# First modulation weights by column halves, sample rows as passes of their own on split weights, smaller transfers at the stage ends, and no table of delays, in a one-core decoder step

## The chip, the cores and the metric

The kernel runs on one core of a Trainium2 chip. The metric is the time of one execution in device microseconds (us). The core has TensorE (PE, with its weight loads shown apart as PEld), VectorE (DVE), ScalarE (ACT), GpSimd (POOL) and SyncE (SP); almost all transfers between DRAM and SBUF are issued on SP's queue.

## The reference, cut to what matters

One layer of a decoder is computed for a prompt of 2,048 tokens and for 8 decode samples of one token each, in float32. D is 1,024 and the FFN is 2,816 wide.

```python
mod = silu(c) @ w_ada + b_ada                 # c: 1 prompt row and 8 sample rows; w_ada is 1024 x 6144
sh1, sc1, ga1, sh2, sc2, ga2 = split(mod, 6)  # parts 0 to 5
h = rmsnorm(x, g_norm1) * (1 + sc1) + sh1
qkv, z, beta, a, aq, ak, av, iq, ik, iw = split(h @ w_in)     # w_in is 1024 x 3664
o_gdn = gated_delta_rule(silu(conv4(qkv)), a, beta)           # chunks of 64 tokens, 4 heads
o_att = attend(aq, ak, av, topk=256 of relu(iq . ik) * iw)    # 4 heads, 2 kv heads
x = x + ga1 * (concat(rmsnorm(o_gdn) * silu(z), o_att) @ w_out)
h2 = rmsnorm(x, g_norm2) * (1 + sc2) + sh2
gate, up = split(h2 @ w_ffn_in)
x = x + ga2 * ((silu(gate) * up) @ w_ffn_out)
y = rmsnorm(x, g_final)
```

The outputs are y for the prompt and for the samples, the new keys, values and index keys, and the new states of the convolution and of the delta rule.

## The kernel before, in words

**Products.** Every float32 product is made of three matmuls on operands that are split into a high and a low part: `mm3` (L206 to L208) issues high by high, high by low and low by high into one bank of PSUM. A weight tile of 128 x 512 is loaded raw into `wr` by `weights` (L175 to L199; the DMA is L188), copied to its high part on ACT (L189) and subtracted to its low part on DVE (L190); both parts lie in `wi`. The split tiles of w_in are written to DRAM (`kept`) in the first group and read from there in the three later ones. The banks of PSUM have names: `d` (four, the large products), `s` and `g` (two each).

**Tokens and groups.** The prompt is worked on in four groups of 512 tokens (`GT`), its 1,024 channels in eight blocks of 128 (`KB`, the index k). The samples ride along: in the projection of group 0, and in the FFN of the last group.

**Two phases.** Phase 1 goes through the groups: `project` (L676 to L768) makes the projection, `narrow` (L771) the per-head decay and index keys from a narrow product `smT`, and the chunks of the delta rule follow. Phase 2 (`phase2`, L1563) does the sparse attention (`indices` L1611, the searches for the top keys, `attends`), the samples' attention and `ffn` (L1784 to L2074). The FFN of a group is w_out, the norm, w_ffn_in by eleven pairs of 256 columns and w_ffn_out; the last group's stands alone at the end.

**Who sets the order.** PE takes the matmuls in the order in which they are written: `o` ties each matmul to the one before. That order comes from `weave` (L518), which runs several generators side by side: in phase 1 the delta rule (`chain`), the per-token work (`toks`) and the large products (`feeds`); in phase 2 `samples`, `indices`, `attends` and `feeds`. Each step of a generator yields its cost on PE, a time to wait before its next step, and the banks it uses. A planner's clock chooses the next step by those numbers. The table `DELAY` adds to that clock: for each generator it holds step numbers with a delay in us, 246 entries, 399 us in total (`feeds` 179, `chain` 69, `attends` 60, `samples` 41, `toks` 36, `indices` 14). It puts no wait into the program; it moves a step back in the order.

**The start.** `modulation` (L322) and `modulate` (L362) load the rows of w_ada for the shift and the scale (parts 0 and 1): eight DMAs of 128 x 1,024 for each (L347), with x of group 0 (L664) between them. The constants, the gate weights and the narrow weights follow on SP's queue (L360, L471 to L489), then the first w_in tiles. Each half of a part takes eight matmuls of 9 columns into two tiles of PSUM, which are copied to SBUF and turned by four times two matmuls (L388) that add the two tiles up; DVE adds the bias (L390). `hidden_T` (L436 to L445) turns x and applies scale and shift, k by k.

**The samples.** In the first three column blocks of group 0's projection the samples are the moving operand: two matmuls of 40 columns for each m and k (L714). In the other four blocks they are the stationary operand and the weight tile moves: two matmuls of 512 columns for each k (`mm_s`, L222 and L223). In the last group's FFN the raw weight tile is used, not the split one: `beside` (L1845) issues four matmuls, each with 32 columns of samples as stationary operand and 128 columns of the weight tile moving, into four strips of one bank. `tick` places them after a k-step. A ring of eight raw tiles (`wr`, `kT`, `V`) carries the weights there. `rows_s` (L1774) lays the samples' gates out to match.

**The stage ends.** The index keys are loaded by eight DMAs of 128 x 512 at the head of phase 2 (L1571). In a group's FFN x after w_out is stored to `x2_d` in one DMA of 2 MB (L1928), when w_out is done, and read again after the first columns of w_ffn_in (L2004). At the end `close` (L1969) scales the four token blocks by the last norm, 1,024 columns at a time on DVE, and stores each; then the samples are scaled and stored by four DMAs (L2073, L2074).

Of the kernel before, what the change touches and what calls it, by code (L numbers as in the profile page):

```python
# [20 lines left out]
try:  # L21
# [9 lines left out]
OP = mybir.AluOpType  # L31
# [32 lines left out]
DELAY = {  # L64
    "attends": {7: 1.43, 11: 5.06, 17: 0.31, 18: 6.69, 19: 0.55, 27: 0.49, 42: 13.11, 51: 1.2, 77: 3.19, 80: 2.39, 103: 0.94, 104: 0.27,
        105: 1.67, 124: 2.19, 125: 0.42, 126: 2.25, 135: 2.33, 137: 2.82, 138: 0.62, 144: 0.42, 149: 0.9, 150: 1.26, 151: 0.57, 152: 0.99,
        252: 0.46, 265: 1.77, 267: 1.16, 275: 0.26, 294: 1.69, 296: 0.59, 301: 1.84},
    "chain": {5: 0.24, 7: 1.06, 16: 2.03, 17: 0.26, 18: 1.33, 19: 0.98, 42: 0.55, 43: 1.2, 44: 0.61, 45: 0.44, 46: 1.05, 48: 0.61, 54: 0.55,
# [6 lines left out]
    "feeds": {1: 3.32, 161: 0.9, 166: 0.74, 242: 0.32, 281: 0.59, 362: 1.55, 363: 0.44, 365: 0.32, 425: 1.19, 431: 4.52, 503: 0.89, 538:  # L75
# [63 lines left out]
class K:  # L139
# [35 lines left out]
    def weights(self, src, key=None, raw=False):  # L175
# [6 lines left out]
        if raw:  # L182
            wr = raw()
        else:
            wr = self.wp.tile([128, 512], F32, name="wr", tag="wr", bufs=WR)
# [136 lines left out]
    def modulation(self):  # L322
# [20 lines left out]
        for part in range(2):  # L343
            if part:
                self.x0 = self.load_x(0)
# [1752 lines left out]
```

## Time and profile before

| | before |
|---|---|
| median of 3 runs | 3591.85 us (3581.23 to 3595.12) |
| the profiled execution, its own time | 3578.49 us |
| its span in the profile | 3576.7 us |
| mean granted clock of TensorE | 0.972 |
| busy share of PE, DVE, ACT, POOL | 94%, 58%, 41%, 16% |
| moved by DMA | 549.74 MB, 154 GB/s on average |

The profile is one execution, recorded by the hardware. A row of the timeline has the start, the duration, the engine, the line of the kernel, the operation, the output and the inputs with their shapes, and how often it stood there; in brackets is the idle time before it and what ended it. "x8" on a row means eight such instructions back to back under one stamp. "SPq" is the issue of a DMA on SP, "DMA" a transfer. A row of the waits has the waiting group, what it waited for, the us lost, how often, and the longest. Matmul ends are modelled, so the distance between two starts says more than a duration.

### The profile page before, as it was taken

Reading aid. Unit: us, or ns where it says so; the run is one execution under the profiler, and the core shown is the slowest. Engines: PE = TensorE matmul, PEld = TensorE weight load, DVE = VectorE, ACT = ScalarE, POOL = GpSimd, SP = SyncE. Lnnn points to the kernel's source line nnn. Section 1 sums busy time; section 2 is a strip of 40 time slices with the busy share of each in tenths; the row PEclk is TensorE's granted clock in tenths of the full one; section 3 lists DMA queues with packets and bytes.
Section 4 is the critical chain, followed back from the end, with each engine's and each line's share of the span. In section 5 each row is a group of like instructions: output and inputs, shape, how many; then the busy total and the mean of one; then the engine's idle time right before and its main releaser. Section 6 shows DMA issues by size and latency. Waiting matters only on the chain.

```text
span 3576.7 us, 62419 instructions
## 1 busy us (share of the span) xinstructions
PE 3367.3 (94%) x23125; PEld 2600.4 (73%) x23125; DVE 2065.2 (58%) x4465; ACT 1462.6 (41%) x2836; POOL 582.6 (16%) x550
## 2 busy tenths in 40 slices
PE   8999999999987889999999999999899999999997
PEld 5877777767765667777776777777677777677775
DVE  3656645636733657666678556667775744444434
ACT  3434323423432333454566545446564533322222
POOL 1001000101000113212220122222021122222223
PEclk8999999999998989999999999999999999999999
DMA  7765754765776344555464454235333333422222
GB/s 264 248 225 170 264 182 152 229 230 165 232 254 207 96 129 134 150 166 165 123 204 146 145 149 139 86 113 202 126 95 93 96 110 106 155 89 80 79 84 67
DMA packets 416877, 549.74 MB, mean 154 GB/s; under 512 B 49860, under 2 KB 287785, under 8 KB 416554
## 3 DMA queue, kind: packets, MB, share of 16 engines
q1 hardware_dynamic: 416562, 545.65, 48.0%
q8 instruction: 184, 3.01, 0.4%
q14 instruction: 131, 1.07, 0.1%
HBM read 441.78 MB, written 122.70 MB: 158 GB/s over the span
## 4 chain that ended last, share of the span: by engine, by line
PE 55%; DVE 5%; issue 3%; DMA 3%; ACT 2%; SPq 1%; POOL 1%; another core or an unknown queue 0%; DVEq 0%; ACTq 0%; POOLq 0%
PE d L206 14%; PE d L208 13%; PE d L207 13%; PE s L1665 3%; PE g L1727 3%; PE s L1710 2%; PE g L1845 1%; PE g L1739 1%; DVE wi L190 1%; ACT bias L1539 1%; DMA wr<-in_w_ffn_in_dram 1%; DMA wr<-in_w_ffn_out_dram 1%; ACT wi L189 1%; DMA x_d<-xt 1%; PE g L1395 0%
## 5 line engine op out<-in xcount | busy, mean ns | idle before, releaser
L206 PE MATMUL d<-hh,wi 128*128 128x512 f32 x1792 | 779.3, 435 | 23.7 <-DVE ca L2011 7.7
L207 PE MATMUL d<-hl,wi 128*128 128x512 f32 x1792 | 708.8, 396 | 2.6 <-DVE hl L445 2.5
L208 PE MATMUL d<-hh,wi 128*128 128x512 f32 x1792 | 709.1, 396 | 0.0
L190 DVE TENSOR_TENSOR wi<-wr,wi 128x512 fp32r<-128x512 f32 x537 | 407.7, 759 | 449.0 <-ACT wi L189 425.0
L189 ACT CAST wi<-wr 128x512 fp32r<-128x512 f32 x537 | 331.9, 618 | 769.8 <-PE d L208 537.3
L206 PEld LDWEIGHTS d<-hh,wi 128*128 128x128 f32 x1792 | 341.7, 191 | 127.9 <-issue 34.9
L208 PEld LDWEIGHTS d<-hh,wi 128*128 128x128 f32 x1792 | 340.8, 190 | 78.0 <-DVE wi L190 0.5
L207 PEld LDWEIGHTS d<-hl,wi 128*128 128x128 f32 x1792 | 342.7, 191 | 74.3 <-issue 11.9
L206 PE MATMUL d<-wi,hh 128*128 128x512 f32 x768 | 330.9, 431 | 19.2 <-DMA wi<-kept 9.9
L206 PE MATMUL d<-wi,ah 128*128 128x512 f32 x704 | 303.4, 431 | 18.5 <-DVE tm L1802 7.8
L208 PE MATMUL d<-wi,hl 128*128 128x512 f32 x768 | 303.9, 396 | 0.0
L207 PE MATMUL d<-wi,hh 128*128 128x512 f32 x768 | 303.5, 395 | 0.4 <-DVE wi L190 0.2
L208 PE MATMUL d<-wi,al 128*128 128x512 f32 x704 | 280.8, 399 | 2.5 <-POOL al L2015 2.5
L207 PE MATMUL d<-wi,ah 128*128 128x512 f32 x704 | 279.4, 397 | 0.0
L2015 POOL TENSOR_TENSOR al<-ca,ah 128x512 fp32r<-128x512 f32 x88 | 122.0, 1395 | 923.4 <-ACT ah L2014 688.3
L1667 ACT ACTIVATE rl<-s 128x512 f32<-128x512 f32 (+3 forms) x288 | 151.0, 543 | 134.3 <-PE s L1665 112.2
L1674 DVE SCALAR_TENSOR_TENSOR sc<-rl,iw,sc 128x512 f32<-128x512 f32 (+3 forms) x224 | 166.0, 741 | 62.2 <-ACT rl L1667 56.8
L1803 POOL TENSOR_TENSOR xt<-xt,tm 128x512 f32<-128x512 f32 x96 | 135.9, 1428 | 367.5 <-DVE tm L1802 293.2
L206 PEld LDWEIGHTS d<-wi,hh 128*128 128x128 f32 x768 | 146.2, 190 | 62.9 <-DMA wi<-kept 9.6
L1539 ACT ACTIVATE bias<-sc,sv 128x640 bf16<-128x640 f32 (+11 forms) x120 | 169.8, 1415 | 39.8 <-DVE sv L1541 29.4
L1665 PE MATMUL s<-ik,iqT 128*128 128x512 f32 (+3 forms) x576 | 168.6, 390 | 16.9 <-DMA kT<-kT_d 13.4
L206 PEld LDWEIGHTS d<-wi,ah 128*128 128x128 f32 x704 | 134.3, 191 | 63.8 <-issue 17.2
(536 smaller groups left out, 5419.6 us busy)
## 6 DMA issues: line engine op xcount, KB each, us to landing
wi<-kept SPq DMA_DIRECT2D x168, 512.0 KB
wr<-in_w_ffn_in_dram SPq DMA_DIRECT2D x572, 128.0 KB
wr<-in_w_ffn_out_dram SPq DMA_DIRECT2D x143, 256.0 KB
kept<-wi SPq DMA_DIRECT2D x56, 512.0 KB
xt<-in_x_prompt_dram SPq DMA_DIRECT2D x8, 2048.0 KB
row<-in_w_ada_dram SPq DMA_DIRECT2D x32, 512.0 KB
wr<-in_w_in_dram SPq DMA_DIRECT2D x56, 256.0 KB
kT<-kT_d SPq DMA_DIRECT2D x54, 256.0 KB
```

Of the source, the lines that this page charges most:

```text
L189: nc.scalar.copy(w[:, 0], wr)
L190: nc.vector.tensor_tensor(w[:, 1], wr, w[:, 0].bitcast(F32), op=OP.subtract)
L206: self.o(nc.tensor.matmul(out, wh, xh, start=start, stop=False, **kw))
L207: self.o(nc.tensor.matmul(out, wh, xl, start=False, stop=False, **kw))
L208: self.o(nc.tensor.matmul(out, wl, xh, start=False, stop=stop, **kw))
L1539: nc.scalar.activation(c, s, AF.Sign, bias=t, accum_out=cnt)
L1665: self.o(nc.tensor.matmul(ps[:, :w], iq[:, h, :].bitcast(F32R), B["ikT"][c * 2 + a][:, :w].bitcast(F32R), start=a == 0, stop=a == 1))
L1667: nc.scalar.activation(r[:, :w], ps[:, :w], AF.Relu)
L1674: nc.vector.scalar_tensor_tensor(s, r[:, :w], iw, s, op0=OP.mult, op1=OP.add)
L1727: self.o(nc.tensor.matmul(po[:, :256], V[:, kb % 4, :], PT[:, b * 256:(b + 1) * 256], start=kb == 0, stop=kb == i))
L1803: (nc.vector if soon else nc.gpsimd).tensor_tensor(xt, xt, tm, op=OP.add)
L2015: nc.gpsimd.tensor_tensor(al[b], a, ah[b].bitcast(F32), op=OP.subtract)
```

## The change

**The start.** The first two parts of w_ada are loaded by halves of their columns (`load_ada`): the first 512 columns of both, four k-blocks to a DMA, go ahead of and between the DMAs of x; the second 512 (`second_half`) are issued after the second w_in tile of the projection. Constants and gate weights that the first steps do not read, and the narrow weights, move behind that. The modulation of the second halves is made inside the projection: its matmuls (`mod_mul`) after step k=1, its turns (`mod_turn`) after step k=2. Low and high k-blocks now add up in PSUM there, and on DVE in the later parts, so that a turn takes four matmuls instead of eight.

**Samples.** In the first three column blocks the samples become the stationary operand as in the others (`mm_s`), and `channels` turns the result back to columns. In the last FFN they also take `mm_s` on the split weights: two matmuls of 512 columns take the place of the four narrow ones. Split tiles there come from a ring that alternates `wi` with the pair `kT` and `V`; the raw ring becomes `wr`, `rl`, `PT`. The samples' rows lie in 8 partitions; `gate`, `outs` and `turn` are rewritten for that. At the ends of w_out and of w_ffn_out the samples' part is taken in after the first and the second token block.

**Parts of transfers.** The index keys are loaded by `keys` when `indices` reaches blocks 4, 6 and 10. x2 is stored by halves of its columns, the second half by token blocks. In the last FFN the closing norm's weight is multiplied in on POOL per half, or taken on DVE with the scaling; ACT scales the first 512 columns and DVE the second, with a DMA for each, and the samples need one DMA.

**No table.** `DELAY` and its use are gone. Nothing else in the planner's costs is changed but what belongs to the new steps.

The diff, cut:

```diff
-DELAY = {
-    "attends": {7: 1.43, 11: 5.06, 17: 0.31, 18: 6.69, 19: 0.55, 27: 0.49, 42: 13.11, 51: 1.2, 77: 3.19, 80: 2.39, 103: 0.94, 104: 0.27,
...
             w = next((w for w in able if w["early"] and self.spent >= self.share()), able[0])
...
-            w["late"] = w["delay"].get(w["steps"], 0.0)
-            w["steps"] += 1
...
                 self.step(w, *said[:2], **(said[2] if len(said) > 2 else {}))
-                w["at"] += w["late"]
...
     def modulation(self):
+        self.load_ada(hh, 0, 0, 0, KB)
...
-        for part in range(2):
-            if part:
-                self.x0 = self.load_x(0)
-            for k in range(KB):
-                nc.sync.dma_start(self.ada[part][k], A["w_ada"][0, k * 128:(k + 1) * 128, part * D:(part + 1) * D])
+        for t in range(4):
+            nc.sync.dma_start(self.x0[:, t, :], A["x_prompt"][0, t * 128:(t + 1) * 128, :])
+        self.load_ada(hl, 1, 0, 0, KB)
...
+    def load_ada(self, to, part, hf, k0, n):
+        c0 = part * D + hf * 512
+        for k in range(0, n, 4):
+            m = min(4, n - k)
+            r0 = (k0 + k) * 128
+            self.nc.sync.dma_start(to[:, k:k + m, :], self.A["w_ada"][0, r0:r0 + m * 128, c0:c0 + 512].rearrange("(a p) c -> p a c", a=m))
...
+    def mod_mul(self, part, hf, tag):
+        pm = self.ps.tile([128, 512], F32, name=tag, tag=tag, bufs=2)
+        for k in range(KB):
+            j = k % 4 * 32
+            self.o(nc.tensor.matmul(pm[j:j + 32], self.cT[:, k, :], self.ada[part][hf][k], start=k < 4, stop=k >= 4, skip_group_check=True))
...
+    def mod_turn(self, part, hf, got, tag):
+        for m in range(4):
+            self.o(nc.tensor.matmul(pt[:, m * 32:m * 32 + 32], got[:, m * 128:(m + 1) * 128], self.f4, start=True, stop=True))
...
     def modulate(self, part):
+                if a:
+                    nc.vector.tensor_tensor(got, got, pm, op=OP.add)
+                else:
+                    got = self.m("m9")[:, :512]
+                    nc.scalar.copy(got, pm)
...
             for m in range(4):
-                for a in range(2):
-                    self.o(nc.tensor.matmul(pt[:, m * 32:m * 32 + 32], got[a][:, m * 128:(m + 1) * 128], self.f4, start=a == 0, stop=a == 1))
+                self.o(nc.tensor.matmul(pt[:, m * 32:m * 32 + 32], got[:, m * 128:(m + 1) * 128], self.f4, start=True, stop=True))
...
     def project(self, g, rows):
+                if samp and not c and k == 1:
+                    self.second_half()
+                if samp and not c and k == 3:
+                    self.narrow_weights()
+                    self.late_consts()
...
-                    if samp:
-                        for part, w in enumerate((wh, wl)):
-                            self.o(nc.tensor.matmul(pq[:, m * 40:m * 40 + 40], w[:, s], hs[:, k, :], start=part == 0 and k == 0 and m == 0,
-                                             stop=part == 1 and k == KB - 1, skip_group_check=True))
-                    yield 3 * MM + samp * 0.12, 0
+                    yield 3 * MM, 0
+                if samp:
+                    self.mm_s(pq, hs[:, k, :], wh, wl, k == 0, k == KB - 1)
+                    yield 2 * MM, 0
+                if samp and not c and k == 1:
+                    for part in range(2):
+                        held.append(self.mod_mul(part, 1, "g"))
+                    yield 3.5, 0
+                if samp and not c and k == 2:
+                    for part in range(2):
+                        self.mod_turn(part, 1, held[part], "g")
+                    self.sample_half(1, raw, hs)
...
+    def channels(self, c, t):
+        for m in range(4):
+            self.o(nc.tensor.transpose(pt[:, m * NS:(m + 1) * NS], t[:NS, m * 128:(m + 1) * 128], self.id[:NS, :NS]))
...
     def indices(self, B):
+            self.keys(*{4: (0, 1), 6: (2,), 10: (3,)}.get(i, ()))
...
     def ffn(self, g):
         def raw():
-            tag = ("wr", "kT", "V", "kT", "wr", "V", "kT", "V")[ring[0] % 8]
+            tag = ("wr", "rl", "PT")[ring[0] % 3]
...
+        def pair():
             ring[0] += 1
+            if ring[0] % 2:
+                w = wp.tile([128, 2, 512], F32R, name="wi", tag="wi", bufs=WI)
+                return w[:, 0], w[:, 1]
+            return [q.tile([128, 512], F32R, name=tag, tag=tag, bufs=KR) for tag in ("kT", "V")]
...
-        def beside(pq, x, wr, start, stop):
-            def run():
-                for j in range(4):
-                    self.o(nc.tensor.matmul(pq[j * 32:j * 32 + 32, :128], x, wr[:, S(j)], start=start, stop=stop, skip_group_check=True))
-            side.append((0, run, 0.3))
+        def beside(pq, x, wh, wl, start, stop):
+            side.append((None, lambda: self.mm_s(pq, x, wh, wl, start, stop), 2 * MM))
...
                 shut(t)
+                if t == 0:
+                    yield from tick()
+                    outs(pq, hf)()
+                    self.squares(ms[:NS, 4], xs, NS)
...
                 gated_add(pd[t], row[:, cs], xt[:, t, cs], hf, t)
+                if hf:
+                    nc.sync.dma_start(self.x2_d[g * GT + t * 128:g * GT + (t + 1) * 128, cs], xt[:, t, cs])
...
-        if not samp:
-            nc.sync.dma_start(self.x2_d[tok].rearrange("(t p) d -> p t d", p=128), xt)
+            if not samp and not hf:
+                nc.sync.dma_start(self.x2_d[tok, cs].rearrange("(t p) d -> p t d", p=128), xt[:, :, cs])
...
-        yield 0, 4 if samp else 20, dict(act=3, dve=4, need="s")
+        yield 0, 4 if samp else 10, dict(act=3, dve=4, need="s")
...
         def close(t):
+            nc.scalar.activation(xt[:, t, :512], xt[:, t, :512], AF.Copy, scale=r)
+            nc.sync.dma_start(to[:, :512], xt[:, t, :512])
+            nc.vector.scalar_tensor_tensor(xt[:, t, 512:], xt[:, t, 512:], r, gf[0][:, 512:], op0=OP.mult, op1=OP.mult)
+            nc.sync.dma_start(to[:, 512:], xt[:, t, 512:])
...
                     finish(t, pd[t])
+                    if t == 1:
+                        yield from tick(True)
+                        outs(pq, hf)()
+                        self.squares(ms[:NS, 4], xs, NS)
+                        sums()
```

How it moves instructions, at three places. First, SP's queue at the start, from the first w_ada load to the first w_in tiles. Before, where L347 loads w_ada, L664 loads x, and L360 to L489 load constants, gate weights and narrow weights:

```order
10 L347 DMA hh<-in_w_ada_dram 128x1024 x4
11 L347 DMA sq<-in_w_ada_dram 128x1024
12 L347 DMA ct<-in_w_ada_dram 128x1024 x2
13 L347 DMA wi<-in_w_ada_dram 128x1024
14 L664 DMA xt<-in_x_prompt_dram 128x4x1024
15 L347 DMA hl<-in_w_ada_dram 128x1024 x4
16 L347 DMA sq<-in_w_ada_dram 128x1024
17 L347 DMA ct<-in_w_ada_dram 128x1024 x2
18 L347 DMA wi<-in_w_ada_dram 128x1024
19 L360 DMA cr<-in_cf_dram 128x1224
```

The same place now, where L342 loads w_ada, L319 x, L322 the samples and L166 the raw w_in tiles:

```order
10 L319 DMA xt<-in_x_prompt_dram 128x1024 x4
11 L342 DMA hl<-in_w_ada_dram 128x4x512 x2
12 L322 DMA row<-in_x_sample_dram 8x1024
13 L166 DMA wr<-in_w_in_dram 128x512 x2
14 L342 DMA sq<-in_w_ada_dram 128x2x512
15 L342 DMA ct<-in_w_ada_dram 128x3x512 x2
16 L342 DMA sq<-in_w_ada_dram 128x2x512
17 L342 DMA ct<-in_w_ada_dram 128x3x512 x2
18 L362 DMA cf<-in_cf_dram 128x450
```

The first two w_in tiles now stand ahead of half of w_ada (rows 14 to 17) and of the constants.

Second, PE in the last FFN, at the end of one k-step (`x_...` is the samples' operand, `wi`, `kT` and `V` weight tiles, `ah` and `al` or `hh` and `hl` the split activations). Before:

```order
10994 L206 MATMUL d<-wi,ah 128x512
10995 L207 MATMUL d<-wi,ah 128x512
10996 L208 MATMUL d<-wi,al 128x512
10997 L1845 MATMUL g<-kT,x_32993 32x128 x4
10998 L206 MATMUL d<-wi,ah 128x512
```

Now:

```order
11062 L186 MATMUL d<-hh,wi 128x512
11063 L200 MATMUL g<-wi,x_32151 40x512
11064 L201 MATMUL g<-wi,x_32151 40x512
11065 L184 MATMUL d<-hh,kT 128x512
11066 L185 MATMUL d<-hl,kT 128x512
```

The four narrow matmuls between two k-steps have become two wide ones, on the split tile that the k-step before them has used.

Third, PE in the inverse of the delta rule's chunks in the last group (`Dm`, `Y` and `E` are the inverse's blocks). Before, with two triples of the projection (L206 to L208) between its steps:

```order
3798 L1041 MATMUL g<-Dm,Y 32x32 x32
3799 L206 MATMUL d<-wi,hh 128x512
3800 L207 MATMUL d<-wi,hh 128x512
3801 L208 MATMUL d<-wi,hl 128x512
3802 L206 MATMUL d<-wi,hh 128x512
3803 L207 MATMUL d<-wi,hh 128x512
3804 L208 MATMUL d<-wi,hl 128x512
3805 L1028 MATMUL g<-Dm,E 32x32 x32
```

Now, where L1092 is the old L1041, L1079 the old L1028 and L1087 the old L1036:

```order
3651 L1092 MATMUL g<-Dm,Y 32x32 x32
3652 L1079 MATMUL g<-Dm,E 32x32 x32
3653 L1087 MATMUL g<-Y,Dm 32x32 x32
3654 L1092 MATMUL g<-Dm,Y 32x32 x32
3655 L1079 MATMUL g<-Dm,E 32x32 x32
```

Steps of the inverse that had two triples between them now follow each other at once. In the same way, in group 1, 65 triples' matmuls stood between the turn of `smT` in `narrow` and its next matmul (L816), and 53 stand there now (L867).

More of the change, by code (lines that the diff above doesn't have):

```diff
@@ L173, in split, with weights @@
         return hi, lo
-    def weights(self, src, key=None, raw=False):
+    def weights(self, src, key=None, raw=None, pair=None):
         nc = self.nc
-        w = self.wp.tile([128, 2, 512], F32R, name="wi", tag="wi", bufs=WI)
+        if pair is None:
+            w = self.wp.tile([128, 2, 512], F32R, name="wi", tag="wi", bufs=WI)
+            hi, lo = w[:, 0], w[:, 1]
+        else:
+            hi, lo = pair()
         if key in self.kept:
@@ L181, in weights @@
             return w[:, 0], w[:, 1]
-        if raw:
+        if raw is not None:
             wr = raw()
@@ L328, in modulation @@
         p, q, c9 = self.p, self.p1, self.c9
+        hh, hl = [p.tile([128, KB, GT], F32R, name=x, tag=x, bufs=1).bitcast(F32) for x in ("hh", "hl")]
+        self.ada = [[[x[:, k, :] for k in range(KB)]] for x in (hh, hl)]
+        self.load_ada(hh, 0, 0, 0, KB)
         vec = q.tile([128, 512], F32, name="gzc", tag="gzc", bufs=2)[:, :128]
@@ new lines, in narrow_weights @@
+    def narrow_weights(self):
+        nc, A, p = self.nc, self.A, self.p1
+        wi = A["w_in"][0].rearrange("(k p) c -> p k c", p=128)
+        for a in range(2):
+            r, k4 = self.m("wsr")[:, :320].rearrange("p (k c) -> p k c", k=4), slice(a * 4, a * 4 + 4)
+            nc.sync.dma_start(r[:, :, 0:8], wi[:, k4, C_BA:C_BA + 8])
+            nc.sync.dma_start(r[:, :, 8:80], wi[:, k4, C_IK:C_IK + 72])
+            nc.scalar.copy(self.wsh[:, k4], r)
+            nc.gpsimd.tensor_tensor(self.wsl[:, k4], r, self.wsh[:, k4].bitcast(F32), op=OP.subtract)
@@ L495, in phase1 @@
         for part in range(2):
-            for _ in self.modulate(part):
-                pass
+            self.mod_turn(part, 0, self.mod_mul(part, 0, "g"), "g")
         self.ordered = True
@@ L505, in stream @@
     def stream(self, run, early=False):
-        name = run.gi_code.co_name
-        return dict(run=run, at=self.now, until=None, early=early, need=None, late=0.0, steps=0, delay=DELAY.get(name, {}))
+        return dict(run=run, at=self.now, until=None, early=early, need=None)
     def busy(self, first, **work):
@@ L688, in project @@
         if samp:
-            xs = p.tile([128, D], F32, name="row", tag="row", bufs=RB)[:NS]
-            nc.sync.dma_start(xs, A["x_sample"][:, 0, :])
-            self.squares(ms[:NS, 4], xs, NS)
-            hs = self.norm_T_s(self.p1, xs, ms[:NS, 4:5], self.A1, B1, "s", 2)
+            self.squares(ms[:NS, 4], self.xs0, NS)
+            raw, hs = self.sample_rows(self.xs0, ms[:NS, 4:5])
+            self.sample_half(0, raw, hs)
+            held = []
         hidden(0)
@@ L1583, in phase2, with keys @@
             self.groups(True)
+    def keys(self, *groups):
+        for g in groups:
+            for a in range(2):
+                self.nc.sync.dma_start(self.ikT[g * 2 + a], self.ikT_d[a, :, g * GT:(g + 1) * GT])
     def groups(self, general):
@@ L1776, in rows_s @@
         nc = self.nc
-        pt = self.ps.tile([128, 512], F32, name="g", tag="g", bufs=2)
-        for k in range(8):
-            j = k % 4 * 32
-            self.o(nc.tensor.matmul(pt[j:j + NS, k // 4 * 128:k // 4 * 128 + 128], self.mod[:, base + k, 1:9], self.id, start=True, stop=True))
-        for j in range(0, 128, 32):
-            nc.scalar.copy(row[j:j + NS], pt[j:j + NS, :256])
+        for hf in range(2):
+            pt = self.ps.tile([128, 512], F32, name="g", tag="g", bufs=2)
+            for k in range(4):
+                self.o(nc.tensor.transpose(pt[:NS, k * 128:(k + 1) * 128], self.mod[:, base + hf * 4 + k, 1:9], self.id))
+            nc.scalar.copy(row[:, hf * 512:(hf + 1) * 512], pt[:NS])
     def ffn(self, g):
```

325 lines of the change are left out of this document (164 added, 161 removed), and 12 rows, old and new, of the table DELAY.

## Prediction

> **What bounds the kernel now.** I read the page first, then a table of stages, then PE's own waits. The page's first lines:
>
> ```profile
> span 3576.7 us, 62419 instructions
> PE 3367.3 (94%) x23125; PEld 2600.4 (73%) x23125; DVE 2065.2 (58%) x4465; ACT 1462.6 (41%) x2836; POOL 582.6 (16%) x550
> ```
>
> PE is busy for 94% of the span and no other engine comes near. So a microsecond of PE work saved is a microsecond of time wherever PE does not wait, and 3576.7 - 3367.3 = 209 us of waiting can shrink or grow. Four windows show where they lie (columns: stretch, then busy us and instructions of PE, PEld, DVE, ACT, POOL, then the granted clock, DMA share and GB/s):
>
> ```profile
> 0.00:50.00 50.00, 33.06 (x154) 16.27 (x154) 11.21 (x26) 17.98 (x44) 9.04 (x25) 0.86 0.87 313
> 1100.00:1350.00 250.00, 206.44 (x2635) 165.26 (x2634) 137.59 (x309) 79.64 (x157) 31.12 (x36) 0.87 0.42 133
> 3120.00:3546.00 426.00, 424.78 (x2615) 304.49 (x2613) 176.28 (x279) 114.36 (x203) 90.74 (x75) 1.00 0.26 79
> 3559.00:3577.00 18.00, 1.47 (x42) 1.01 (x42) 9.72 (x20) 4.55 (x16) 5.80 (x7) 0.59 0.32 124
> ```
>
> The start waits for data (DMA share 0.87), the change of phase at 1100 to 1350 loses 44 us, the last FFN is pure PE work (424.8 of 426), and the last 18 us hold no PE work to speak of. The change touches all four.
>
> **The start.** Stamps of the first weights, of the scale and shift, and of the first two steps of the first projection (PE L206 is the first of a matmul triple):
>
> ```profile
> 4.14 1.85 SPq L347 DMA_DIRECT2D hh<-in_w_ada_dram  x4
> 28.00:32.00 4.00, 4.00 (x18) 2.14 (x18) 2.56 (x6) 2.31 (x7) 0.85 (x2) 0.50 1.03 411
> 36.07 1.32 SPq L188 DMA_DIRECT2D wr<-in_w_in_dram  x2
> 46.60 0.19 DVE L390 TENSOR_TENSOR mod<-s,cv 128x36 f32<-128x36 f32 x1
> 49.51 0.79 PE L206 MATMUL d<-hh,wi 128*128 128x512 f32 x1 [0.70 <-ACT hh L444]
> 57.26 0.48 PE L206 MATMUL d<-hh,wi 128*128 128x512 f32 x1
> 61.35 0.48 PE L206 MATMUL d<-hh,wi 128*128 128x512 f32 x1
> ```
>
> Before the first w_in tile the queue holds 8.4 MB of w_ada and 2.1 MB of x; they run at 411 GB/s. Steps k=0, 1, 2 begin at 49.51, 57.26 and 61.35; step 0 is slow because the clock is at half.
>
> As the change section's rows of SP show, half of w_ada has moved behind x and behind the first two w_in tiles; the small constants have moved behind it too. Ahead of the scale and shift now lie 6.3 MB: at 0.411 MB/us 15.4 us, so from 2 us (one DMA fewer in front) plus some 2 us to land it is about 20, where the same bytes took until about 36. The chain from there (matmuls, copy, turn, L390, hidden) took 12.5 us in the old order, where L390 was queued behind a weight split; I take 7 to 8, so the first triple is at 27 to 28. Steps 0 and 1 at half clock (about 7 us each as at 49.51, less for the shorter sample work) end near 40. Step 2 needs the other 4.2 MB, 1.6 MB of constants, gate weights and one kept tile, and its own tile: some 12.6 MB in all, 31 us, so about 35 to landing, 38 to 41 with the smaller packets, and 2 more to be split. The second halves' matmuls stand before it on PE as well. I put step 2 at 43 against 61.35: **18 us saved** (10 if the queue delivers at the 313 GB/s of the first window; 21 at best). By the Trainium skill, DMA: Bandwidth & Descriptors (Specifications), a core gets about 358 GB/s from HBM; by that step 2 would be some 5 us later. The 411 GB/s of the window is above it, so I keep the window.
>
> **The first projection.** The rest of the m-step that begins at 61.35, and a sample pair of the later form (L222, L223, moving 512 columns):
>
> ```profile
> 62.13 0.29 PE L714 MATMUL s<-hs,wi 128*128 128x40 f32 x2
> 62.27 0.48 PE L206 MATMUL d<-hh,wi 128*128 128x512 f32 x1
> 204.46 0.40 PE L223 MATMUL s<-wi,hs 128*40 128x512 f32 x1
> 204.69 0.40 PE L206 MATMUL d<-wi,hh 128*128 128x512 f32 x1
> 204.93 0.39 PE L207 MATMUL d<-wi,hh 128*128 128x512 f32 x1
> 44.05 1.02 PE L453 MATMUL s<-cf,row 8*128 8x8 f32 x8
> ```
>
> A 512-column matmul takes 0.23 us from start to start, so the two 40-column ones cost 0.92 - 3 x 0.23 = 0.23 per m, 0.92 per k. The row pass costs 2 x 0.23 = 0.46. 22 steps are left after the two counted above: 22 x 0.46 = 10.1; against it 12 small transposes at 1.02/8 = 0.13, 1.6. **8.5 us** (6.5 to 8.5); folds and copies go beside PE work.
>
> **Later modulations.** Adding the two halves on DVE instead of in PSUM drops 4 turn matmuls from each of 8 turns, two records each:
>
> ```profile
> 20.09 1.75 PE L388 MATMUL s<-cf,m 128*128 128x32 f32 x14 [0.68 <-ACT m L383]
> ```
>
> 64 x 1.75/14 = **8 us** (3 if most stand where PE waits anyway). The added DVE step takes the place of an ACT copy.
>
> **Samples in the last FFN.** One k-step, from the second matmul after the sample group to the same one a step later:
>
> ```profile
> 3211.15 0.42 PE L1845 MATMUL g<-V,x 128*32 128x128 f32 x8
> 3211.84 0.39 PE L207 MATMUL d<-hl,wi 128*128 128x512 f32 x1
> 3214.14 0.39 PE L208 MATMUL d<-hh,wi 128*128 128x512 f32 x1
> 3214.46 0.43 PE L1845 MATMUL g<-kT,x 128*32 128x128 f32 x8
> 3215.15 0.39 PE L207 MATMUL d<-hl,wi 128*128 128x512 f32 x1
> 3558.91 0.16 PEld L1845 LDWEIGHTS g<-wr,x 128*32 128x32 f32 x8 [0.36 <-issue]
> 3559.04 0.24 PEld L1845 LDWEIGHTS g<-kT,x 128*32 128x32 f32 x8
> 3559.26 0.24 PEld L1845 LDWEIGHTS g<-V,x 128*32 128x32 f32 x8
> ```
>
> In the change section's rows of PE, four 32-column matmuls have become two passes of 512. The step is 3215.15 - 3211.84 = 3.31; twelve matmuls at 0.23 are 2.76, so the group costs 0.55 and the pair 0.46. With 16 + 88 + 44 = 148 steps: 148 x 0.09 = **13 us** (8 to 16). Here the Trainium skill, TensorEngine Tiling (Array Packing), speaks against the change: its Overview gives operands of at most 32 columns up to four times the speed when tiled. Its Key Properties say, too, that a change of tiling mode drains the engine. The rows show both: groups back to back follow each other at 0.22 us (3559.04 to 3559.26), a lone group between full matmuls costs 0.55. By the first sentence alone the passes would lose 148 x 0.24 = 36 us; the step decides. The deeper ring of split tiles replaces one of raw tiles, and the windows leave DVE and ACT idle over half of this stage, so it hides.
>
> **Phase change, x2, tail.** Waits of PE and the transfers behind them:
>
> ```profile
> PE s L1665 <- DMA kT<-kT_d: 13.4, 1, 13.4
> 1313.36 0.33 SPq L1571 DMA_DIRECT2D ik<-ikT_d  x1
> 1318.99 0.65 SPq L1657 DMA_DIRECT2D iqT<-iqT_d  x1
> 1241.53 9.31 DMA x_d<-xt
> 3558.58 0.40 PE L208 MATMUL d<-wi,al 128*128 128x512 f32 x1
> 3566.59 1.28 DVE L1969 SCALAR_TENSOR_TENSOR xt<-xt,rnz,row 128x1024 f32<-128x1024 f32 x1
> 3568.80 3.17 SPq L2074 DMA_DIRECT2D out_dram<-sc  x4
> ```
>
> Four of the eight index-key loads leave the head of the queue: 2 of the 4 us that lie between 1313.4 and 1319, plus 1 MB at 411 GB/s, overlapping: **3 us** (0 to 5). The x2 store of 2 MB held the chain 9.31 us; half now goes a projection half earlier and the rest in four pieces, so the last piece waits for some 3 us: 6 at this place, about 0 where other streams cover it: **6 us** (0 to 12). At the end the last triple is at 3558.6 and the span ends 17.7 us after it. Four full-width scalings (1.28 each), then the samples' scaling and four DMAs, become half-width work on ACT and DVE with the samples taken in before t=2; I count four gated adds, four halves and 4 us for samples on DVE, ending 8 us after PE, and 3 to 4 us to land: **6 us** (3 to 8). At the end of w_out the same sample work stands ahead of the hidden states: **2 us lost** (0 to 4).
>
> **The table of delays.** The diff removes 246 entries, 399 us in total, which had moved steps of the streams back. Where a step comes earlier than its operand, PE waits in order and all behind it. Two places, in rows:
>
> ```profile
> 386.12 0.40 PE L816 MATMUL s<-gt,cf 128*128 128x16 f32 x2 [0.31 <-DVE gt L809]
> 1234.74 0.75 PE L1041 MATMUL g<-Dm,Y 32*32 32x32 f32 x64
> 1236.11 0.45 DVE L1042 COPY_PREDICATED Dm<-cl,g 128x256 f32<-128x256 uint8 x1
> 1237.03 0.75 PE L1028 MATMUL g<-Dm,E 32*32 32x32 f32 x64
> ```
>
> L816 waits for a row of small DVE steps and is in time to 0.3 us. Between the turn of smT and it stood 65 triples' matmuls, now 53 in the same group: 12 x 0.23 = 2.8 us of cover gone. The other place is the chain's inverse in the last group, the change section's last rows: the six matmuls that stood between L1041 and L1028 (L1092 and L1079 now) have gone. Dm is written 1.8 us after L1041 begins, so L1079 will wait about a microsecond. Going along both orders this way, I find cover shorter than the slack at some fifteen steps of chain, narrow and samples, 22 us in all, and longer where PE waited now at others, 10 us; at the ends of FFN groups some 80 us less cover and 70 more. The rest of the gaps are of the same size, since the planner's own waits give most of them. Net 22, and I add 6 for the half clock that follows a stall (0.87 in the second window): **28 us lost**, bounds -10 (the old delays no longer fit) and +95 (a quarter of 399).
>
> **Sum.** 18 + 8.5 + 8 + 13 + 3 + 6 + 6 - 2 = 60.5 saved, 28 given back: 32.5. The profiled execution took 3578.5 us, so 3546 on its scale. It lies 13.4 under the median of the three runs, 3591.85, and on that scale the forecast is **3559 us**.
>
> **Rivals.**
> - *The delays were needed.* The streams then stall again wherever the table had moved them. It decides from 60.5 us on; at the upper bound of 95 us the time is 3591.9 + 34.5 = 3626. For it: PE takes everything in written order, and counted as above L816 loses its cover in three groups, 2 to 5 us each. Against: nearly all gaps are as long as they were. Between 42 and 78 us it reads as no change. Slower by over 0.5% (from 78 us on): 0.13.
> - *The start stays bound by the queue*, step 2 waiting for everything as before: 18 less, 3577, no measurable change. The same bytes must come before step 2; against it, the 411 GB/s leave no room for 61 us. 0.07.
> - *The tiled form was cheap.* Mode changes that the passes still pay, so a pair at 0.79 instead of 0.46: 13 us gained become 36 lost, 3608. The pairs at 204.46 already stand between full matmuls and cost 0.23 each. 0.03.
> - *The table cost nothing:* 3531. 0.15.
>
> The forecast's own case has 0.55; the remaining 0.07 are milder returns of stalls, near 3580. About 0.5% is what a measurement of this kernel can tell from no change, so faster means under 3574 and slower over 3610: 0.70, 0.17, 0.13. The range takes in a free table with the gains at their upper bounds (3591.9 - 78) and stalls of 78 us: 3514 to 3610.
>
> **What would show it.** Step k=2 of the first projection near 43 us; a k-step of the last FFN at 3.22 instead of 3.31; 11 to 12 us from the last triple to the end; L867 (the old L816) waiting 2 to 5 us in three groups; PE busy some 30 to 40 us less. If PE's idle time between 100 and 3050 us grows by over 60, the first rival is right; if step 2 stands past 55, the second.

## The result, and the profile after

| | before | changed |
|---|---|---|
| median of 20 runs each | 3584.57 us (3574.69 to 3595.66) | 3604.66 us (3596.99 to 3627.46) |
| span of the profiled execution | 3576.7 us | 3605.8 us |

The ratio is 1.0057 (95% interval 1.0044 to 1.007): the change made the kernel 20 us slower, where the forecast was 32.5 us faster. With more runs the median of before has come down from 3591.85 to 3584.57. The ratios below are against the kernel before as it ran beside each experiment, and leave out one execution of 8,168 us (the carried-over table) and one of 12,557 us (the old FFN), more than twice as long as all others.

The page of the changed kernel, its first lines:

```profile
span 3605.8 us, 60166 instructions
PE 3362.7 (93%) x21994; PEld 2601.9 (72%) x21994; DVE 2122.1 (59%) x4502; ACT 1472.4 (41%) x2855; POOL 593.4 (16%) x539
```

PE's work went down by 1131 instructions but its busy time by only 4.6 us, and the rest of the span, in which PE waits, went from 209 to 243 us.

Both kernels have the same 9792 matmuls of the large products (L206 to L208 before, L184 to L186 now), twelve to a k-step, in the same order. So the time at which the n-th k-step begins shows where time comes and goes. The table is counted from the traces; its last column belongs to an experiment below, the kernel before with an empty table of delays.

| k-step | where | before | changed | before, no table |
|---|---|---|---|---|
| 0 | first projection | 49.5 | 30.5 | 50.0 |
| 2 | | 61.4 | 43.7 | 61.0 |
| 32 | group 0, after z | 185.0 | 182.2 | 185.7 |
| 96 | group 1 | 491.1 | 515.8 | 513.1 |
| 224 | first step of group 0's w_out | 1159.9 | 1181.3 | 1177.0 |
| 384 | phase 2, FFN of group 1 | 1876.5 | 1897.7 | 1908.3 |
| 512 | the same | 2415.7 | 2452.4 | 2490.3 |
| 672 | last w_out | 3069.0 | 3099.4 | 3137.6 |
| 815 | last k-step, its last matmul | 3558.6 | 3587.5 | 3628.0 |

The start gains 18 us, as forecast. Then the changed kernel loses 15 us by step 32, another 28 by step 96, and in phase 2 some 15 more between steps 384 and 512. The kernel without a table loses in two of these stretches too, 21 us between steps 32 and 96 and 43 between 384 and 512, and 15 more between 224 and 384.

Steps 0 and 2 of the first projection in the changed kernel's timeline:

```profile
30.45 0.80 PE L184 MATMUL d<-hh,wi 128*128 128x512 f32 x1 [0.70 <-ACT hh L488]
...
43.65 0.48 PE L184 MATMUL d<-hh,wi 128*128 128x512 f32 x1
```

What follows the first projection's second column block, on ACT and PE (L207 is the samples' fold, L943 and L944 empty a bank of the projection, L944 frees it):

```profile
113.77 0.39 PE L201 MATMUL s<-wi,hs 128*40 128x512 f32 x1
...
114.20 0.58 ACT L207 COPY fold<-s 8x512 f32<-8x512 f32 x1 [0.72 <-PE s L201]
...
114.89 0.59 ACT L943 COPY raw<-d 128x512 f32<-128x512 f32 x1
...
117.61 0.38 ACT L944 COPY hist<-d 128x3 f32<-128x3 f32 x4
117.85 0.80 PE L184 MATMUL d<-hh,wi 128*128 128x512 f32 x1 [3.69 <-ACT hist L944]
```

The fold stands ahead of the four banks on ACT, and needs the samples' pass, which is PE's last work of the block. So no bank is emptied before PE has finished, and the first becomes free only with the four L944 that stand behind all the copies. PE waits 3.7 us for it, at 118 us and again at 151.

The first decay matmul of `narrow` in group 0 (L867), and the matmuls behind it:

```profile
97.24 0.58 PE L867 MATMUL s<-gt,cf 128*128 128x16 f32 x2 [3.95 <-issue]
...
98.65 0.63 PE L185 MATMUL d<-hl,wi 128*128 128x512 f32 x1
99.08 0.63 PE L186 MATMUL d<-hh,wi 128*128 128x512 f32 x1
```

and PE's waits at the same line in two more groups (us in total, times, longest):

```profile
PE s L867 <- DVE gt L860: 3.3, 1, 3.3
PE s L867 <- ACT dec L1590: 3.2, 1, 3.2
```

The first wait is 3.95 us, and the matmuls after it follow each other at 0.43 us instead of 0.23. All three waits were forecast (2 to 5 us).

Samples in the last FFN: the first passes of a w_ffn_out half, then the pairs of two k-steps in w_ffn_in:

```profile
3216.41 0.40 PE L200 MATMUL g<-wi,x 128*40 128x512 f32 x1
...
3217.58 0.40 PE L201 MATMUL g<-wi,x 128*40 128x512 f32 x1
3217.82 0.39 PE L184 MATMUL d<-kT,ah 128*128 128x512 f32 x1
...
3236.80 0.40 PE L200 MATMUL g<-wi,x 128*40 128x512 f32 x1
...
3240.01 0.39 PE L200 MATMUL g<-kT,x 128*40 128x512 f32 x1
```

From pair to pair a k-step of w_ffn_in takes 3.21 us, as forecast (3.22; it was 3.31). But where the samples' work comes in a row, three pairs take 1.41 us, while three of the old groups would take about 0.55 + 2 x 0.22 = 0.99, an estimate from the lone group's price and the rows quoted for 3559. In the trace of before 22 of the 148 groups stand directly behind another one.

The end of the kernel:

```profile
3582.71 1.75 DVE L1858 TENSOR_TENSOR xt<-xt,tm 128x512 f32<-128x512 f32 x1
...
3583.86 6.35 POOL L2140 TENSOR_TENSOR xt<-xt,row 128x512 f32<-128x512 f32 x4
...
3584.38 0.68 DVE L1857 TENSOR_TENSOR tm<-d,row 128x512 f32<-128x512 f32 x1
...
3587.49 0.40 PE L186 MATMUL d<-kT,al 128*128 128x512 f32 x1
...
3599.81 0.38 SPq L2033 DMA_DIRECT2D out_dram<-xt  x1
```

From the end of the last triple to the end of the span 17.9 us pass, against 17.7 before. The change of phase:

```profile
1338.59 0.59 PE L1329 MATMUL g<-cf,s 24*128 24x24 f32 x4 [2.59 <-DMA s<-in_state_conv_dram]
...
1345.06 1.22 PE L1721 MATMUL s<-ik,iqT 128*128 128x512 f32 x2 [4.93 <-DMA iqT<-iqT_d]
```

PE waits 2.6 and 4.9 us there, where it waited 13.4 us before.

### The profile page after: what moved, and what is told of

Same layout as the page of the kernel before. It is cut to its first block, busy times and chain, and to the rows that moved or that the text cites. A ratio compares the mean times of both kernels' runs of the same rounds, so it can differ in the third digit from the quotient of the medians.

```text
span 3605.8 us, 60166 instructions
## 1 busy us (share of the span) xinstructions
PE 3362.7 (93%) x21994; PEld 2601.9 (72%) x21994; DVE 2122.1 (59%) x4502; ACT 1472.4 (41%) x2855; POOL 593.4 (16%) x539
## 4 chain that ended last, share of the span: by engine, by line
PE 53%; DVE 6%; issue 3%; ACT 2%; DMA 2%; SPq 1%; POOL 1%; DVEq 0%; ACTq 0%; POOLq 0%
PE d L184 13%; PE d L186 13%; PE d L185 12%; PE s L1721 3%; PE s L1766 3%; PE g L1783 3%; PE g L1795 1%; DVE wi L168 1%; PE g L200 1%; PE g L201 1%; DMA wr<-in_w_ffn_in_dram 1%; DMA wr<-in_w_out_dram 1%; ACT bias L1590 1%; ACT wi L167 0%; DVE ca L1857 0%
## 5 line engine op out<-in xcount | busy, mean ns | idle before, releaser
L184 PE MATMUL d<-hh,wi 128*128 128x512 f32 x1616 | 694.8, 430 | 26.5 <-DVE tm L1857 6.3
L185 PE MATMUL d<-hl,wi 128*128 128x512 f32 x1616 | 643.8, 398 | 5.3 <-DVE hl L489 5.1
L168 DVE TENSOR_TENSOR wi<-wr,wi 128x512 fp32r<-128x512 f32 x525 | 396.1, 755 | 419.6 <-ACT wi L167 413.9
L186 PE MATMUL d<-hh,wi 128*128 128x512 f32 x1616 | 643.0, 398 | 0.0
L184 PEld LDWEIGHTS d<-hh,wi 128*128 128x128 f32 x1616 | 310.6, 192 | 122.4 <-issue 21.0
L185 PEld LDWEIGHTS d<-hl,wi 128*128 128x128 f32 x1616 | 311.2, 193 | 75.8 <-issue 10.1
L186 PEld LDWEIGHTS d<-hh,wi 128*128 128x128 f32 x1616 | 310.0, 192 | 69.8 <-DVE wi L168 0.4
L184 PE MATMUL d<-wi,hh 128*128 128x512 f32 x736 | 317.3, 431 | 19.1 <-DMA wi<-kept 11.5
L185 PE MATMUL d<-wi,hh 128*128 128x512 f32 x736 | 292.2, 397 | 0.4 <-DVE wi L168 0.4
L186 PE MATMUL d<-wi,hl 128*128 128x512 f32 x736 | 291.7, 396 | 0.3 <-issue 0.3
L184 PE MATMUL d<-wi,ah 128*128 128x512 f32 x616 | 263.4, 428 | 9.2 <-ACT ah L2102 5.4
L186 PE MATMUL d<-wi,al 128*128 128x512 f32 x616 | 245.2, 398 | 2.5 <-POOL al L2103 2.5
L185 PE MATMUL d<-wi,ah 128*128 128x512 f32 x616 | 244.2, 396 | 0.0
L1858 POOL TENSOR_TENSOR xt<-xt,tm 128x512 f32<-128x512 f32 x96 | 141.2, 1482 | 401.3 <-DVE tm L1857 339.3
L184 PEld LDWEIGHTS d<-wi,hh 128*128 128x128 f32 x736 | 140.7, 191 | 64.1 <-DMA wi<-kept 16.2
L186 PEld LDWEIGHTS d<-wi,hl 128*128 128x128 f32 x736 | 140.5, 191 | 32.2 <-issue 0.3
```

The costliest lines, as they stand in the source:

```text
L168: nc.vector.tensor_tensor(lo, wr, hi.bitcast(F32), op=OP.subtract)
L184: self.o(nc.tensor.matmul(out, wh, xh, start=start, stop=False, **kw))
L185: self.o(nc.tensor.matmul(out, wh, xl, start=False, stop=False, **kw))
L186: self.o(nc.tensor.matmul(out, wl, xh, start=False, stop=stop, **kw))
L1858: (nc.vector if soon else nc.gpsimd).tensor_tensor(xt, xt, tm, op=OP.add)
```

## The experiments

Theory T: the table of delays was worth far more than the 28 us of the forecast, and the other parts gain about what was forecast. Theory O: the table is worth about 28 us, and the new parts bring stalls of their own.

**The table alone.** The kernel before, with nothing else changed:

```diff
-DELAY = {
-    "attends": {7: 1.43, 11: 5.06, 17: 0.31, 18: 6.69, 19: 0.55, 27: 0.49, 42: 13.11, 51: 1.2, 77: 3.19, 80: 2.39, 103: 0.94, 104: 0.27,
...
+DELAY = {}
```

> The kernel before with the table of delays emptied and nothing else changed. Theory T (the table was needed; all other parts gain about what was forecast, some 55 to 60 us, and the table's loss eats them and 20 us more): 65 to 85 us slower than before, ratio 1.018 to 1.024. Theory O (the table is worth about the 28 us of the forecast, and the rest of the shortfall of some 50 us is stalls that the new parts bring themselves): 20 to 35 us slower, ratio 1.006 to 1.010.

Measured: 1.0207 (1.0185 to 1.0229), 74 us slower. Its page:

```profile
span 3646.1 us, 62431 instructions
PE 3389.1 (93%) x23125; PEld 2612.8 (72%) x23125; DVE 2064.7 (57%) x4465; ACT 1461.0 (40%) x2836; POOL 583.9 (16%) x550
```

PE has the same 23125 matmuls as before. It waits 257 us instead of 209, and is busy 22 us longer with the same work. The mean granted clock is 0.966 instead of 0.972, and 3367.3 x 0.972 / 0.966 = 3388, so the lower clock is enough for these 22 us. Theory T holds: the other parts of the change take 1.0207 down to 1.0057, 54 us, and the table that went with them was worth 74.

**The old table in the changed kernel.** Each entry was carried to the step that corresponds to its old one, 237 of 246 entries, 375 of 399 us.

```diff
+    "toks": {5: 2.25, 12: 2.32, 14: 0.55, ...
...
+            w["late"] = w["delay"].get(w["steps"], 0.0)
...
+                w["at"] += w["late"]
```

> The changed kernel with the table back, each entry moved to the step that corresponds to its old one (237 of 246 entries, 375 of 399 us). Theory T: 60 to 80 us faster than the changed kernel, so 40 to 60 us faster than before, ratio 0.983 to 0.989. Theory O: 20 to 35 us faster than the changed kernel, ratio to before 0.996 to 1.001. Since the entries were made for another order, a gain under 15 us would say that a table does not carry over.

Measured: 1.0035 (1.0017 to 1.0052), some 8 us faster than the changed kernel, with intervals that just overlap. This is neither theory's number; it is the third case that the text names, a table that does not carry over.

**Its entries for phase 1 alone** (against the kernel with the carried-over table; the entries of `feeds` behind step 1156 go too):

```diff
-    "attends": {7: 1.43, ...
-    "indices": {12: 1.72, ...
-    "samples": {0: 4.78, ...
```

> The changed kernel with the old table's entries for phase 1 alone (120 entries, 141 us). With the whole old table the trace ran 25 to 40 us ahead at the change of phase and gave 15 to 30 back in phase 2. Theory T: phase 1 is alike in both kernels, so its entries still fit, phase 2's don't: 15 to 30 us faster than the changed kernel, ratio to before 0.997 to 1.002. Rival S: the lead at the change of phase is work put off to phase 2, and comes back: 5 to 10 us faster, as with the whole table, ratio 1.003 to 1.004.

Measured: 1.0061 (1.0043 to 1.0079), no gain at all, and neither expectation. In its trace k-step 256 begins 42 us earlier than in the changed kernel and the last one 5 us earlier. Rival S takes the lead for work put off. The traces show little of that: when step 256 begins, PE has done only 36 other matmuls fewer (9234 against 9270), and ACT and DVE 6 and 10 us less of work. The lead is lost between steps 256 and 672, where PE waits 103 us against 73. So these entries do save time in phase 1, and phase 2 without its entries loses it again; why is not shown. A lead at one k-step says little about the time at the end.

**The same delays at other steps.** The kernel before, each key of its table raised by ten:

```diff
-    "toks": {2: 2.25, 9: 2.32, 11: 0.55, ...
+    "toks": {12: 2.25, 19: 2.32, 21: 0.55, ...
```

> The kernel before with the same table of 399 us, but every entry ten steps later in its stream. Theory T (what counts is the step at which a delay stands): 55 to 95 us slower than before, as with no table or worse, ratio 1.015 to 1.027. Rival S (the table's sum keeps the streams apart, and the place matters little): under 30 us slower, ratio under 1.008.

Measured: 1.0136 (1.0113 to 1.0159), 49 us slower. It lies between the two expectations, nearer to T: two thirds of what the table is worth are lost when the same delays stand ten steps later.

**The fold behind the convolutions:**

```diff
+            for m in range(4):
+                self.conv(g, c * 4 + m, pd[m])
             if samp:
                 self.queue.append(self.channels(c, self.fold(pq, to=self.m("fold"))))
-            for m in range(4):
-                self.conv(g, c * 4 + m, pd[m])
```

> The changed kernel with the samples' fold written behind the four convolutions at the end of each of the first three column blocks of group 0, so that ACT empties the four banks of the projection first. Theory O: PE's waits of 3.7 us at 114 and 147 us go to under 1 us, with the half clock after them, and the time falls by 8 to 15 us, ratio to before 1.001 to 1.004. Theory T: no more than 3 us, since what is saved early is waited for later.

Measured: 1.0023 (1.0012 to 1.0035), 12 us faster than the changed kernel. So theory O is right for this part. The same block end now:

```profile
108.54 0.58 ACT L943 COPY raw<-d 128x512 f32<-128x512 f32 x1
...
109.02 0.16 ACT L944 COPY hist<-d 128x3 f32<-128x3 f32 x1
...
109.23 0.19 PEld L184 LDWEIGHTS d<-hh,wi 128*128 128x128 f32 x1 [0.60 <-ACT hist L944]
...
111.19 0.58 ACT L207 COPY fold<-s 8x512 f32<-8x512 f32 x1
```

The first bank is emptied as soon as its own matmuls end, each L944 follows its L943, the fold comes last, and PE's weight load waits 0.60 us.

**One planner number for the three waits of L867:**

```diff
-        yield 0, 12
+        yield 0, 17
```

> The changed kernel with one number of the planner raised, the wait before the first decay matmul in narrow from 12 to 17 us. Theory T: the three waits of 3.2 to 4.0 us at L867 go, with the half clock after them, and the time falls by 10 to 16 us, ratio to before 1.001 to 1.003. Theory O: the waits go too, but the order behind them shifts and gives half of it back, 3 to 8 us.

Measured: 1.004 (1.0025 to 1.0055), some 6 us faster, with intervals that overlap, as theory O expects. The three waits, 10.4 us in all without the slow clock behind them, are gone in the trace; PE still waits 244 us in all, against 243, so as much waiting came up elsewhere.

**New tables.** To the kernel with the late fold, a table made from its own profile: each wait of PE over 0.2 us becomes a delay of that length at the step before the one that waited. A second and a third pass add the waits that are left.

```diff
+DELAY = {
+    "attends": {7: 0.74, 18: 3.17, 27: 1.37, ...
```

> The changed kernel with the late fold and a new table: every wait of PE over 0.2 us in the profile of the kernel with the late fold became a delay of the same length at the step before the one that waited (155 entries, 198 us). Theory T (a table is worth its stalls, but only for the order that it was made from): 30 to 60 us faster than the kernel with the late fold, ratio to before 0.985 to 0.994. Rival S (a delay moves a stall to the next place, and one pass over one trace settles nothing): within 10 us of it, ratio 0.999 to 1.005.

> The first new table's kernel with a second pass: the waits of PE over 0.2 us that its own profile still shows are added to the table in the same way (254 entries, 383 us). Theory T (a table approaches its worth pass by pass, since each pass only fits the order that it was made from): 10 to 25 us faster than the first pass, ratio to before 0.990 to 0.994. Rival S (passes only move stalls about): within 5 us of the first pass, ratio 0.9955 to 0.998.

> A third pass on the changed kernel with the late fold (332 entries, 575 us), from the second pass's profile. Theory T (passes converge; the first two gave 20 and 12 us): 4 to 10 us faster than the second pass, ratio to before 0.9905 to 0.9925. Rival S (delays past the second pass begin to cost as much as they save): 0.993 or above.

Measured: 0.9968 (0.9952 to 0.9983), 0.9935 (0.9921 to 0.995) and 0.9918 (0.9892 to 0.9945). The first pass gave 20 us, between the two expectations, the second 12 and the third 6, both as T expects; the last two intervals overlap. The third is the fastest kernel of the study, 29 us faster than before. The second pass's page:

```profile
span 3559.8 us, 60149 instructions
PE 3332.4 (94%) x21994; PEld 2579.1 (72%) x21994; DVE 2114.0 (59%) x4502; ACT 1474.3 (41%) x2855; POOL 584.0 (16%) x539
```

PE waits 227 us instead of the changed kernel's 243, and is busy 30 us less for the same 21994 matmuls. The kernel with the late fold, from which the tables were made, stands between:

```profile
span 3587.1 us, 60169 instructions
PE 3352.8 (93%) x21994; PEld 2593.5 (72%) x21994; DVE 2117.8 (59%) x4502; ACT 1474.2 (41%) x2855; POOL 594.1 (17%) x539
```

So two passes took 7 us from the waits, which they were made from, and 20 us from PE's busy time. The granted clock went from 0.971 to 0.975; how much of the 20 us that is was not measured.

**The same on the kernel before:** one pass on its profile without a table, and one further pass on top of its own table.

```diff
-    "attends": {7: 1.43, 11: 5.06, 17: 0.31, 18: 6.69, ...
+    "attends": {17: 0.27, 21: 0.67, 42: 4.31, 51: 0.96, ...
```

> The kernel before without its table, and one pass of a new one made in the same way from that kernel's own profile (149 entries, 226 us). Theory T: like the changed kernel, it gets some 20 to 35 us of its 74 back in one pass, ratio 1.010 to 1.015; then what the changed kernel lacks is passes, not something of its own. Rival S: over 50 us come back, ratio under 1.007, so that the changed kernel's smaller gain has a cause in the change itself.

> The kernel before with one further pass on top of its own table (316 entries, 547 us). If its table had converged: within 6 us of before, ratio 0.998 to 1.002, and the changed kernel's gain with new tables is due to the change's other parts. If it had not: 10 us faster or more, ratio under 0.997, and that much of the gain of the new tables is the passes' own.

Measured: 1.0053 (1.0039 to 1.0067), so 55 of the 74 us come back in one pass, as rival S expects, while the changed kernel with the late fold got 20; why it got less is not shown. And 1.0137 (1.0106 to 1.0167), 49 us slower, which neither case had: a further pass over the old table takes two thirds of its worth away.

**The old FFN in the changed kernel:** `ffn`, `rows_s` and `weights` as before, all else as changed.

```diff
-            if not samp and not hf:
-                nc.sync.dma_start(self.x2_d[tok, cs].rearrange("(t p) d -> p t d", p=128), xt[:, :, cs])
+        if not samp:
+            nc.sync.dma_start(self.x2_d[tok].rearrange("(t p) d -> p t d", p=128), xt)
...
-        yield 0, 4 if samp else 10, dict(act=3, dve=4, need="s")
+        yield 0, 4 if samp else 20, dict(act=3, dve=4, need="s")
```

> The changed kernel with the old FFN in it (the old sample groups on raw weights, the whole x2 store, the old closing), all else as changed and without the table. By the forecast's terms for these parts (13 + 6 + 6 - 2) it is 23 us slower than the changed kernel, ratio to before 1.012. Rival P (the parts in the last FFN and at the end brought the 0 to 6 us that the two traces show there, and only the x2 store is open): 3 to 10 us slower, ratio 1.0065 to 1.0085.

Measured: 1.0167 (1.0146 to 1.0187), 39 us slower than the changed kernel, more than either expected. Most of it is not in the last FFN: of the 43 us that its last k-step is late, 41 are there at step 672. Its page:

```profile
span 3648.5 us, 61982 instructions
PE 3374.3 (92%) x22897; PEld 2589.4 (71%) x22897; DVE 2073.8 (57%) x4479; ACT 1457.0 (40%) x2828; POOL 584.3 (16%) x549
```

PE waits 274 us instead of 243. One place is the x2 store. PE's waits for the norm's rows there, in the changed kernel, with the old FFN in it, in the kernel before without a table, and in the kernel before:

```profile
PE s L485 <- ACT xt L476: 6.5, 4, 3.0
```

```profile
PE s L485 <- DVE xt L478: 11.8, 1, 11.8
```

```profile
2594.80 0.38 SPq L1904 DMA_DIRECT2D x_d<-xt  x1
...
2605.24 1.42 DVE L410 TENSOR_SCALAR xt<-xt,rnz 128x1024 f32<-128x1024 f32 x2 [3.48 <-DMA x_d<-xt]
...
2606.05 1.14 PE L417 MATMUL s<-cf,xt 128*128 128x128 f32 x3 [14.09 <-DVE xt L410]
```

```profile
PE s L441 <- DVE xt L434: 4.6, 2, 4.0
```

x is scaled in place, so the scaling waits for the store. Without a table the whole store costs one wait of 12 to 14 us; with the table it cost 4.0, since two of its entries (7.99 and 7.6 us, `feeds` steps 2334 and 2336) stand there. The halves of the x2 store and the table cover the same wait. But it is only 12 of the 41 us, and the stretch that holds it, from step 512 to 672, is no longer than in the changed kernel (645 us against 647). The loss lies elsewhere: 12 us between steps 224 and 256, and 30 between 384 and 512, where PE waits 31 us instead of 16, in many places, as it does there in the kernel before without a table (32 us). In the first three groups the edit changes the store and the planner's wait behind it, 20 us instead of 10, and with that the order of all streams. The two were not tested apart, so which of them brings the rest stays open.

**The end.**

```diff
-                            nc.gpsimd.tensor_tensor(xt[:, t, cs], xt[:, t, cs], gf[0][:, cs], op=OP.mult)
+                            nc.vector.tensor_tensor(xt[:, t, cs], xt[:, t, cs], gf[0][:, cs], op=OP.mult)
```

> The changed kernel with one engine changed: the multiplication of the last FFN's first half by the closing norm's weight on DVE instead of POOL. In the changed kernel's trace four such POOL operations take 6.35 us at the end of w_ffn_out, and a DVE operation beside them took 1.75 us where it takes 0.67 alone. If POOL slows DVE there: 14 to 15.5 us from the last triple to the end instead of 18.3, the time 3 to 4 us less. If DVE's own queue is the limit: 18 us or more, no gain.

Measured: 1.0049 (1.0028 to 1.007), the same as the changed kernel within the intervals. The last triple starts at 3583.65 in a span of 3603.9: 20.3 us to the end, where it is 18.3 in the changed kernel. That fits DVE's own queue as the limit there.

## Why the prediction was wrong, point by point

- **The table of delays** was the step that failed: "28 us lost", in the trace of the kernel without it 69 us and in its time 74. The mechanism was right and so were the places that were looked at; the size of this term was not. Two sentences of the working carry the error. "The rest of the gaps are of the same size, since the planner's own waits give most of them": without the table PE waits 48 us more in all, and the forecast had 22. And "some 80 us less cover and 70 more" was netted, although cover that grows where PE did not wait gains nothing; this is argued, not measured by itself. Then the waits cost more than their length: 48 us of them came with 22 us of slower work at the lower clock, where 6 were added for it. The upper bound of 95 held. The rival "the delays were needed" (0.13) is what happened; its point of decision, 60.5, was 54.
- **The sign for that rival** was badly chosen: PE's idle time between 100 and 3050 us grew by only 26 us (165 to 191), not by 60, although the rival was right. Even in the kernel before without a table it grew by only 47, since work at the slow clock counts as busy. The sign of the forecast itself, PE busy 30 to 40 us less, failed too: 4.6.
- **The start**: 17.7 us against 18, step 2 at 43.65 against 43. The number is right, the way to it in part by luck. The first triple stood at 30.45, not at 27 to 28, and the transfers ran at 365 GB/s from 2 to 38 us, not at 411. Against that, steps 0 and 1 took 5.8 and 3.4 us instead of about 7 each; the second halves' matmuls begin behind them at 39.66. The errors cancelled.
- **The first projection**: a k-step fell by 0.42 to 0.48 us as forecast (0.46), some 10 us over 22 steps. "Folds and copies go beside PE work" was wrong: the fold's place on ACT held back the banks and cost 12 us, all of the gain. From step 2 to step 32 the changed kernel takes 138.6 us and the kernel before 123.7; with the late fold it is 124.0, and there PE waits 4.25 us at 72 us for the fold itself (L817, the turn in `channels`). So even then the stretch gained nothing.
- **The last FFN**: 3.21 for a k-step as forecast, but from step 688 to the end 5.3 us are saved, not 13. The price of a lone group was used for all 148; the 22 that stand behind another cost 0.22, as the row at 3559 showed, and a pair costs 0.46 anywhere. So 126 x 0.09 - 22 x 0.24 = 6 was to be expected. The samples' work at the end of w_out cost 4.4 us (steps 682 to 688) against 2.
- **The change of phase**: 5.9 us less waiting against 3. **The end**: nothing against 6; 17.9 us pass after the last triple instead of 17.7, where 11 to 12 were forecast.
- **x2**: 6 us in the forecast, from the 9.31 us of the store in the trace of before, whose table covers most of the wait. Without a table the wait is 12 to 14. With the old FFN back the changed kernel loses 39 us, so the FFN's parts together do more than forecast, but for a kernel without a table, and the planner's number among them.
- **The later modulations**: the turns fell from 128 records on PE, busy for 14.9 us, to 64, busy for 8.7: 6 us of work against 8. How much of it became time was not measured.

What the parts are worth depends on the table beside them: 54 us without any (1.0207 to 1.0057), and 66 with the late fold; with one pass of a new table each, 1.0053 and 0.9968, 30 us; with the best table found for each, 1.0 and 0.9918, 29 us, the late fold included in both. The forecast set the parts' worth, read from a trace with a table, against the loss of that table as if neither depended on the other. They overlap. That the sum of 60.5 came out close to the 54 is partly luck: the terms for the first projection, the last FFN and the end were too large, those for the change of phase and x2 too small.

That new passes would stop at 0.9918 is not shown, nor is why a further pass harms the kernel before.

## What to carry to other kernels

A hand-made order or a table of delays belongs to one program: price its removal by removing it alone, not by counting cover in a trace that it has shaped, and make it anew after any change in the steps. A gain that is read from a trace with such a table holds beside that table; the table and a structural change may cover the same wait. A small piece of work put last on PE and first on the engine that empties the banks can cost as much as the larger piece that it replaces saved.

## What the hardware showed beside this

- After PE's wait of 3.95 us the matmuls ran at 0.43 us from start to start instead of 0.23 until 102.7, some 5 us; the granted clock is 0.50 from 97 to 102 us and 1.00 from 103 on. The Trainium skill, TensorE: Matmul & The Clock Gate (Part 1), says that the array's clock is halved after an idle window of about 3.4 us; the rows agree. Waits of 3.29 and 3.16 us at the same line were followed by 0.43 too, the second after 1.6 us at 0.23, so these rows do not give the window's length.
- At 3582.71 a DVE operation with two inputs in SBUF (L1858) took 1.75 us where it mostly takes 0.68. POOL was at work all that time, first on the same kind of sum and from 3583.86 on the four operations that take 6.35 us. L1857, with one input in PSUM, took 0.68 at 3584.38 beside these. The Trainium skill, GPSIMD Engine Reference (Specifications), has POOL's SBUF interface shared with VectorE when a DVE instruction has two SBUF inputs; the rows agree.
